# Ordering the high parts of weights behind copies and evictions on ScalarE, and the first layer's value columns as single chunks

## The chip, the cores and the metric

The kernel runs on one core of one Trainium2 chip. Five engines work beside each other and meet only through semaphores: TensorE (PE in the profile, with its weight loads as PEld), VectorE (DVE), ScalarE (ACT), GpSimd (POOL) and SyncE (SP, which here only issues DMAs). [...] The metric is the time of one execution on the device in microseconds; the time before is the median of three runs.

## The reference, cut to what matters

Two layers run over 256 positions with a model width of 2048, all in float32. A layer is

```python
proj = rms_norm(x, mix_norm[l]) @ w_in[l]           # 2048 x 7680: q 1024 | k,v 512 | u 1024 | v 1024 | gates 4096
branch_a = sliding_window_attention(rope(q), rope(k), v, sinks[l]) @ w_attn_branch[l]
branch_b = chunked_sgu(gelu(uv), w_spatial[l], ...) @ w_sgu_branch[l]
merged = sigmoid(gates_a) * branch_a + sigmoid(gates_b) * branch_b
x = x + merged @ w_out[l]
h2 = rms_norm(x, ffn_norm[l])
x = x + (silu(h2 @ w_gate[l]) * (h2 @ w_up[l])) @ w_down[l]     # width 5632
```

Nearly all of the arithmetic is the product of 256 rows with weights that are read from memory once.

## The kernel before, in words

**Entries.** The weights are cut into columns of 512 (a chunk) and these into pieces of 256 rows, 512 KB each. A piece is an *entry*: it is loaded by a DMA that SP issues (L199), split by ACT into a rounded high part (`whi`, L222) and by DVE into the rest (`wlo`, L223), and multiplied by PE with the transposed activations, which are split in the same way (`uh`, `ul`). Of the four partial products three are taken, so one 128x256x512 product is six matmuls (L310 to L312 for two values of `kk`). An ordinary entry is multiplied with both halves of the rows and has twelve. There are four buffers each for `whi` and `wlo`; the program splits an entry four places ahead of its use (`W_SPLIT`), so the high part of entry k+4 takes the buffer that entry k gives back.

**Singles and pairs.** A *single* takes one chunk in eight entries (or four, where the inner width is 1024). A *pair* takes two chunks at once and treats one block of them by the Strassen-Winograd scheme: instead of eight products of that block it has seven, P1 to P7, each an entry of six matmuls, six of which are the *head* of the pair. For that DVE forms four differences of weight pieces (L210), and after P5 two copies on ACT have to move banks: `kept<-acc` (L333) and `acc<-acc` (L334, bank a[1] into bank a[0]). P2 adds to a[0] and cannot begin before L334. After P6 and after P7, DVE reads bank a[1] (`kept`, L336), and nothing may be added to a[1] until it has. Later ACT puts the kept sums into the second pair of banks (L339).

**Order on PE.** PE's instructions run in the order in which they are written. The head of a pair is woven into the last entries of the chunk before it. With t the last entries of that chunk and h the head P1, P5, P2, P6, P7, P4, the order is t0 h0 t1 h1 t2 t3 h2 h3 t4 h4 t5 h5. For a pair that follows a chunk of only four entries (the gate chunks 5 and 6, after the first chunk of the spatial branch, once in each layer) it is t0 h0 t1 h1 t2 h2 h3 t3 h4, and h5 comes after the pair's own first entry.

**Order on the other engines.** ACT, DVE and the DMA queues are ordered by the scheduler of the compiler, before anything runs. Work beside the products (norms, rotary, scores, softmax, gelu, transposes) is put in by `after(n, ...)` and comes due at every twelfth matmul or so (`tick`). `tc.issue_after(ins)` binds everything traced inside it to come later than `ins` on the engine of `ins`. A transposition goes by DVE blocks (`box`, L380), sixteen small DMAs (L385, issued by SP for q, k, the attention and the spatial branch, by POOL elsewhere), and copies on ACT that turn the result into `uh` (L403, L407) or `qT` (L703).

**First part of a layer.** The chunks of `w_in` come in the order of `FIRST_PART[l]`. Layer 0: kv, q0, q1, gate 0, each as a single, then the pairs (v0, v1), (gate 1, u0), (u1, gate 2), (gate 3, gate 4). Layer 1 has (q1, gate 0) as a pair too. Finished banks are evicted by ACT: gates, q and kv at L885, u and v at L776.

Of the kernel before, what the change touches and what calls it, by code (L numbers as in the profile page):

```python
# [1 line left out]

# [8 lines left out]
AF = mybir.ActivationFunctionType  # L11
# [35 lines left out]
Q_FIRST = 17  # L47
Q_STEP = 5
LOAD_BY = (1, 3, 4, 4)
FIRST_PART = [[(("kv", 0),), (("q", 0),)] + early + [(("v", 0), ("v", 1)), (("gate", 1), ("u", 0)), (("u", 1), ("gate", 2)),  # L50
              (("gate", 3), ("gate", 4))]
              for early in ([(("q", 1),), (("gate", 0),)], [(("q", 1), ("gate", 0))])]
GELU_A = 0.044715
GELU_C = 0.7978845608028654

# [2 lines left out]
def hybrid_trunk(ctx: ExitStack, tc: tile.TileContext, x, mix_norm, w_in, q_norm, k_norm, sinks,  # L58
                 sgu_ln_g, sgu_ln_b, w_spatial, b_spatial, w_attn_branch, w_sgu_branch, w_out,
                 ffn_norm, w_gate, w_up, w_down, cosine, sine, out):  # L60
    nc = tc.nc
# [15 lines left out]
    def nm(s):  # L77
        names[0] += 1
        return f"{s}_{names[0]}"

    def slot(shape, dt=F32, name="s"):
        return big.tile(shape, dt, tag="s4", name=nm(name))
# [13 lines left out]
    class Plan:  # L96


        def __init__(self, key, head, body):
            self.key, self.head, self.body = key, head, body  # L100
            self.left = len(head) + len(body)
            self.paired = bool(head)
            self.opened, self.acc, self.calls = set(), {}, None
            for e in head + body:
                e["plan"] = self
            for e in body:
                if e["tag"] == "G":
                    self.last_g = e
# [7 lines left out]
    def half(w, h, tag):  # L116
        ld = load_of(w, h)
        return dict(tag=tag, h=h, loads=[ld], src=ld[0])
# [33 lines left out]
    for l in range(DEPTH):  # L152
        wl = w_in[l]

        def of_in(kind, c):
            o = {"kv": O_KV, "q": 0, "v": O_V, "u": O_U, "gate": O_GATE}[kind] + c * CW
            return wl[:, o:o + CW]

        for f in FIRST_PART[l]:
            plans.append((single if len(f) == 1 else pair)(("in", l), *(of_in(*c) for c in f)))  # L160
# [11 lines left out]
    entries = []  # L172
    for p in plans:
        if p.head:
            h, n = p.head, min(6, len(ahead.body))
            t = [entries.pop() for _ in range(n)][::-1]
            if n == 6:
                entries += [t[0], h[0], t[1], h[1], t[2], t[3], h[2], h[3], t[4], h[4], t[5], h[5]]
            else:
                entries += [t[0], h[0], t[1], h[1], t[2], h[2], h[3], t[3], h[4]]  # L180
                p.body.insert(1, h[5])
        entries += p.body
        ahead = p

    class Stream:
# [1 line left out]


        def __init__(self):
            self.raws, self.parts = {}, []  # L190
            self.asked = self.summed = self.at = 0

        def load(self, upto):
# [20 lines left out]
        def split(self, upto):  # L214
            while len(self.parts) < min(upto, len(entries)):
                e = entries[len(self.parts)]
                raw = self.raws[e["src"]]
                hi = wsp.tile([P, 2, CW], F32R, tag="hi", name=nm("whi"))
                lo = wsp.tile([P, 2, CW], F32R, tag="lo", name=nm("wlo"))
                one = len(self.parts) < 2  # L220
                for i in ([slice(0, 1), slice(1, 2)] if one else [slice(0, 2)]):
                    nc.scalar.activation(hi[:, i, :], raw[:, i, :], AF.Copy)  # L222
                    self.last = nc.vector.tensor_tensor(out=lo[:, i, :], in0=raw[:, i, :], in1=hi[:, i, :].bitcast(F32),  # L223
                                            op=ALU.subtract)
                self.parts.append((hi, lo))
# [8 lines left out]
    stream = Stream()  # L234
# [8 lines left out]
    def tick():  # L243
        slot_no[0] += 1
        due = [s for s in steps if s[0] <= slot_no[0]]
        steps[:] = [s for s in steps if s[0] > slot_no[0]]
        for _, fn in sorted(due, key=lambda s: s[0]):
            with tc.issue_after(stream.last.ins):
                fn()
# [39 lines left out]
    def block(units, h, t):  # L289

        k, tt = 2 * (h % 2), slice(t * P, (t + 1) * P)
        return units[h // 2][0][:, k:k + 2, tt], units[h // 2][1][:, k:k + 2, tt]

    def banks(p, which):
        if which not in p.acc:
            other = p.paired and p.key[0] != "in" and which == "a"
            if other or p.key[0] == "in":
                odd[0] = other and not odd[0]
            pool, tag = (ps_at, "at") if other and odd[0] else (ps_acc, "acc")
            p.acc[which] = [pool.tile([P, CW], F32, tag=tag, name=nm("acc")) for _ in range(NT)]  # L300
        return p.acc[which]

    def add_product(p, ps, u, w):

        (uh, ul), (hi, lo) = u, w
        first = id(ps) not in p.opened
        p.opened.add(id(ps))
        for kk in range(2):
            a, b = uh[:, kk, :], ul[:, kk, :]
            nc.tensor.matmul(ps, a, hi[:, kk, :], start=first and kk == 0, stop=False, skip_group_check=True)  # L310
            nc.tensor.matmul(ps, a, lo[:, kk, :], start=False, stop=False, skip_group_check=True)  # L311
            nc.tensor.matmul(ps, b, hi[:, kk, :], start=False, stop=kk == 1, skip_group_check=True)  # L312

    def step():
        e = entries[stream.at]
        p, tag = e["plan"], e["tag"]
        units = units_at[p.key]
        w = stream.next()
        if tag in "XGU":
            ps = banks(p, "b" if tag == "U" else "a")  # L320
            todo = [(ps[t], block(units, e["h"], t)) for t in range(NT)]
        else:
            sh, sl = units[WINO][2:]
            which, t, form = {"P1": ("a", 1, (0, 0)), "P2": ("a", 0, (1, 0)), "P6": ("a", 1, 1), "P7": ("a", 1, 2),
                              "P4": ("a", 1, (1, 1)), "P5": ("a", 0, 0), "P3": ("b", 0, 3)}[tag]
            todo = [(banks(p, which)[t], (sh[:, form], sl[:, form]) if isinstance(form, int)
                     else block(units, 2 * WINO + form[0], form[1]))]
        for ps, u in todo:
            add_product(p, ps, u, w)
        a, b = p.acc.get("a"), p.acc.get("b")  # L330
        if tag == "P5":
            p.kept = slot([P, 2, CW], name="kept")
            nc.scalar.activation(p.kept[:, 1, :], a[0], AF.Copy)  # L333
            nc.scalar.activation(a[0], a[1], AF.Copy)  # L334
        elif tag in ("P6", "P7"):
            nc.vector.tensor_tensor(out=p.kept[:, int(tag == "P7"), :], in0=a[1], in1=p.kept[:, 1, :], op=ALU.add)  # L336
        if "then" in e:
            for t, ps in enumerate(banks(p, "b")):
                nc.scalar.activation(ps, p.kept[:, t, :], AF.Copy)  # L339
                p.opened.add(id(ps))  # L340
        p.left -= 1
        if e is getattr(p, "last_g", None):
            p.calls[0](a)
        if p.left == 0 and p.paired:
            p.calls[1](b)
        debt[0] += len(todo)
        if debt[0] >= 2:
            debt[0] -= 2
            if p.left or p.paired:
                tick()  # L350
# [7 lines left out]
    def product(key):  # L358

        p = run(key)  # L360
        while p.left:
            step()
        return p.acc["a"]
# [151 lines left out]
    norm = Norm(first_cols)  # L515
# [249 lines left out]
    class Spatial:  # L765
# [6 lines left out]
        def half(self, ps, name):  # L772

            dst = slot([P, NT, CW], name=name)
            for t in range(NT):
                nc.scalar.activation(dst[:, t, :], ps[t], AF.Copy, scale=self.nrm.rh[t])  # L776
            return dst

        def gelu(self, dst, t):
# [90 lines left out]
    for l in range(DEPTH):  # L870
# [6 lines left out]
        def taken(kind, c):  # L877

            def by(ps):
                if kind in ("v", "u"):  # L880
                    (spa.v if kind == "v" else spa.u)(c, ps)
                    return
                dst = slot([P, NT, CW], name=kind)
                for t in range(NT):
                    nc.scalar.activation(dst[:, t, :], ps[t], AF.Tanh if kind == "gate" else AF.Copy,  # L885
                                         scale=(norm.rh if kind == "gate" else norm.r)[t])
                if kind == "gate":
                    gates[c] = dst
                else:
                    att.keys(dst) if kind == "kv" else att.queries(c, dst)  # L890
            return by
# [7 lines left out]

        for chunks in FIRST_PART[l]:  # L900
            projected(*chunks)


        for j in range(NCH):
            ps = product(("att", l))
# [8 lines left out]
        for j in range(NCH):  # L914
            if j == 1:
                projected(("gate", 5), ("gate", 6))
            ps = product(("sgu", l))
# [12 lines left out]
        norm = residual(("mix", l), nxt, scale=0.5)  # L930
# [23 lines left out]
        for r, (f0, f1) in enumerate(ROUNDS):  # L954
# [5 lines left out]
            elif l + 1 < DEPTH:  # L960
                norm = Norm(mix_cols(l + 1), True)
# [41 lines left out]
```

## Time and profile before

| what | value |
|---|---|
| median of three runs | 2497.29 us (2497.01 to 2497.77) |
| the profiled execution's own time | 2497.96 us |
| its span, first to last instruction | 2496.3 us |
| PE busy | 2468.9 us, 99% |
| DVE busy | 1950.6 us, 78% |
| ACT busy | 1442.4 us, 58% |
| POOL busy | 286.1 us, 11% |
| mean granted TensorE clock | 0.997 |

The profile comes from one execution. A row of the timeline gives the start, the duration, the engine, the source line, what is written from what, the number of merged instructions, and in brackets how long the engine had been idle before it and what ended the idle time. Matmuls are pipelined: a row's duration of 0.39 us is longer than the distance to the next one.

### The profile page before, as it was taken

To read this page: it belongs to the slowest core of one execution; us is meant where nothing else is said; L and a number is where in the kernel's file an instruction comes from. 1 tells how busy PE (TensorE), PEld (TensorE's weight loads), DVE (VectorE), ACT (ScalarE), POOL (GpSimd) and SP (SyncE) were. 2 spreads that over 40 slices of the span, in tenths; PEclk is the share of its full clock that TensorE was granted. 3 is DMA by queue.
4 is the path that set the end of the run, shared out by engine and by line. 5 is a ranking of instruction groups with operands and counts; after the bars stand their busy time and mean duration, and the time that the engine had idled before them with its cause. 6 is when DMAs were issued, how large, how long until landed. Compare 5 with 4: busy or idle time off the path is not lost.

```text
span 2496.3 us, 31305 instructions
## 1 busy us (share of the span) xinstructions
PE 2468.9 (99%) x11076; PEld 2029.9 (81%) x11076; DVE 1950.6 (78%) x2279; ACT 1442.4 (58%) x1808; POOL 286.1 (11%) x527
## 2 busy tenths in 40 slices
PE   9999999999999999999999999999999999999999
PEld 7788888788888888888888888787888888888887
DVE  6888676787877787778878986767878777877786
ACT  5576544565655565556656665445655555655564
POOL 3100002131110111001101000112211101110110
PEclk9999999999999999999999999999999999999999
DMA  8565567566665757566657546665767566666664
GB/s 292 175 190 166 194 194 223 182 211 219 191 230 170 227 186 233 179 214 205 217 157 247 170 159 222 205 198 181 230 194 223 193 207 196 218 203 192 214 193 151
DMA packets 275661, 502.54 MB, mean 201 GB/s; under 512 B 26224, under 2 KB 36048, under 8 KB 275504
## 3 DMA queue, kind: packets, MB, share of 16 engines
q1 hardware_dynamic: 259472, 484.25, 61.1%
q0 software_dynamic: 15712, 16.01, 2.2%
q8 instruction: 87, 1.43, 0.2%
q14 instruction: 70, 0.57, 0.1%
q10 hardware_dynamic: 320, 0.27, 0.0%
HBM read 475.27 MB, written 2.10 MB: 191 GB/s over the span
## 4 chain that ended last, share of the span: by engine, by line
PE 93%; DVE 4%; issue 1%; ACT 1%; DMA 1%; SPq 0%; DVEq 0%; ACTq 0%
PE acc L310 30%; PE acc L311 30%; PE acc L312 30%; DVE wlo L223 2%; PE po L758 1%; DVE raw L210 1%; PE pt L421 1%; DMA raw<-in_w_in_dram 0%; PE psc L719 0%; SPq L385 0%; PE ppt L748 0%; ACT whi L222 0%; PE psg L836 0%; DVE pr L723 0%; DVE kept L336 0%
## 5 line engine op out<-in xcount | busy, mean ns | idle before, releaser
L223 DVE TENSOR_TENSOR wlo<-raw,whi 128x1024 fp32r<-128x1024 f32 (+1 forms) x1045 | 1272.8, 1220 | 488.9 <-ACT whi L222 474.2
L222 ACT ACTIVATE whi<-raw 128x1024 fp32r<-128x1024 f32 (+1 forms) x1045 | 1103.6, 1058 | 950.6 <-PE acc L312 768.1
L310 PE MATMUL acc<-whi,uh 128*128 128x512 f32 x3094 | 1211.3, 391 | 15.6 <-ACT acc L334 10.8
L311 PE MATMUL acc<-wlo,uh 128*128 128x512 f32 x3094 | 1205.8, 390 | 0.9 <-DVE wlo L223 0.8
L312 PE MATMUL acc<-whi,ul 128*128 128x512 f32 x3094 | 1205.9, 390 | 0.0
L310 PEld LDWEIGHTS acc<-whi,uh 128*128 128x128 f32 x3094 | 581.6, 188 | 138.0 <-ACT acc L334 12.0
L311 PEld LDWEIGHTS acc<-wlo,uh 128*128 128x128 f32 x3094 | 581.8, 188 | 122.6 <-DVE wlo L223 3.0
L312 PEld LDWEIGHTS acc<-whi,ul 128*128 128x128 f32 x3094 | 581.4, 188 | 121.7
L385 POOL DMA_DIRECT2D tt<-box x480 | 235.2, 497 | 1721.5 <-DVE box L380 573.2
L210 DVE TENSOR_TENSOR raw<-raw,raw 128x1024 f32<-128x1024 f32 x196 | 239.1, 1220 | 1.4
L310 PE MATMUL acc<-whi,sh 128*128 128x512 f32 x392 | 158.5, 404 | 4.5 <-DVE kept L336 3.6
L311 PE MATMUL acc<-wlo,sh 128*128 128x512 f32 x392 | 154.3, 394 | 0.8 <-DVE wlo L223 0.8
L312 PE MATMUL acc<-whi,sl 128*128 128x512 f32 x392 | 154.2, 393 | 0.0
L310 PEld LDWEIGHTS acc<-whi,sh 128*128 128x128 f32 x392 | 74.3, 190 | 32.2 <-issue 12.3
L312 PEld LDWEIGHTS acc<-whi,sl 128*128 128x128 f32 x392 | 74.4, 190 | 15.9
L311 PEld LDWEIGHTS acc<-wlo,sh 128*128 128x128 f32 x392 | 74.5, 190 | 15.0 <-DVE wlo L223 1.1
L336 DVE TENSOR_TENSOR kept<-acc,kept 128x512 f32<-128x512 f32 x98 | 67.0, 684 | 0.4 <-PE acc L312 0.4
L339 ACT ACTIVATE acc<-kept 128x512 f32<-128x512 f32 x98 | 56.6, 588 | 9.5 <-DVE kept L336 9.2
L853 DVE SCALAR_TENSOR_TENSOR xs<-acc,xs 128x512 f32<-128x512 f32 (+1 forms) x66 | 41.4, 667 | 7.8 <-PE acc L312 7.8
L942 ACT ACTIVATE hid<-acc,rhalf 128x512 f32<-128x512 f32 x44 | 30.4, 690 | 21.0 <-PE acc L312 21.0
L943 DVE SCALAR_TENSOR_TENSOR hid<-hid,acc 128x512 f32<-128x512 f32 x44 | 29.8, 684 | 9.3 <-ACT hid L942 9.3
L333 ACT ACTIVATE kept<-acc 128x512 f32<-128x512 f32 x49 | 29.1, 595 | 13.0 <-PE acc L312 13.0
(135 smaller groups left out, 885.2 us busy)
## 6 DMA issues: line engine op xcount, KB each, us to landing
raw<-in_w_in_dram SPq DMA_DIRECT2D x239, 512.0 KB, 4.6
raw<-in_w_up_dram SPq DMA_DIRECT2D x176, 512.0 KB, 4.8
raw<-in_w_gate_dram SPq DMA_DIRECT2D x176, 512.0 KB, 4.6
raw<-in_w_down_dram SPq DMA_DIRECT2D x176, 512.0 KB, 4.6
raw<-in_w_out_dram SPq DMA_DIRECT2D x64, 512.0 KB, 4.7
raw<-in_w_attn_branch_dram SPq DMA_DIRECT2D x32, 512.0 KB, 5.4
raw<-in_w_sgu_branch_dram SPq DMA_DIRECT2D x32, 512.0 KB, 4.2
tt<-box POOLq DMA_DIRECT2D x480, 32.0 KB, 4.2
```

The source lines that it names most:

```text
L210: self.last = nc.vector.tensor_tensor(out=self.raws[d], in0=self.raws[x], in1=self.raws[y], op=ALU.subtract)
L222: nc.scalar.activation(hi[:, i, :], raw[:, i, :], AF.Copy)
L223: self.last = nc.vector.tensor_tensor(out=lo[:, i, :], in0=raw[:, i, :], in1=hi[:, i, :].bitcast(F32), op=ALU.subtract)
L310: nc.tensor.matmul(ps, a, hi[:, kk, :], start=first and kk == 0, stop=False, skip_group_check=True)
L311: nc.tensor.matmul(ps, a, lo[:, kk, :], start=False, stop=False, skip_group_check=True)
L312: nc.tensor.matmul(ps, b, hi[:, kk, :], start=False, stop=kk == 1, skip_group_check=True)
L336: nc.vector.tensor_tensor(out=p.kept[:, int(tag == "P7"), :], in0=a[1], in1=p.kept[:, 1, :], op=ALU.add)
L339: nc.scalar.activation(ps, p.kept[:, t, :], AF.Copy)
L385: queue.dma_start(dst[j * B:(j + 1) * B, i], box[i * B:(i + 1) * B, j])
L853: nc.vector.scalar_tensor_tensor(out=xs[:, t, sl], in0=sums[t][:, i * w:(i + 1) * w], scalar=scale, in1=xs[:, t, sl], op0=ALU.mult, op1=AL ...
L942: nc.scalar.activation(th, g[t], AF.Tanh, scale=norm.rh[t])
L943: nc.vector.scalar_tensor_tensor(out=th, in0=th, scalar=1.0, in1=g[t], op0=ALU.add, op1=ALU.mult)
```

## The change

There are three edits. First, the stream of weights remembers an ACT instruction, `stream.urgent`: the last L334 copy, or the last eviction of q, gate, u or v (not of kv). Each high part traced after it (L222) is bound to come behind it on ACT. Second, in layer 0 the value chunks v0 and v1 are two singles instead of one pair. Third, where a pair follows a chunk of four entries, the head begins one entry earlier and ends before the pair's own first entry.

```diff
-FIRST_PART = [[(("kv", 0),), (("q", 0),)] + early + [(("v", 0), ("v", 1)), (("gate", 1), ("u", 0)), (("u", 1), ("gate", 2)),
-              (("gate", 3), ("gate", 4))]
-              for early in ([(("q", 1),), (("gate", 0),)], [(("q", 1), ("gate", 0))])]
+FIRST_PART = [[(("kv", 0),), (("q", 0),)] + early + [(("gate", 1), ("u", 0)), (("u", 1), ("gate", 2)), (("gate", 3), ("gate", 4))]
+              for early in ([(("q", 1),), (("gate", 0),), (("v", 0),), (("v", 1),)],
+                            [(("q", 1), ("gate", 0)), (("v", 0), ("v", 1))])]
...
-                entries += [t[0], h[0], t[1], h[1], t[2], h[2], h[3], t[3], h[4]]
-                p.body.insert(1, h[5])
+                entries += [h[0], t[0], h[1], t[1], h[2], h[3], t[2], h[4], t[3], h[5]]
...
-            self.raws, self.parts = {}, []
+            self.raws, self.parts, self.urgent = {}, [], None
...
-                    nc.scalar.activation(hi[:, i, :], raw[:, i, :], AF.Copy)
+                    with tc.issue_after(self.urgent.ins) if self.urgent else nullcontext():
+                        nc.scalar.activation(hi[:, i, :], raw[:, i, :], AF.Copy)
...
-            nc.scalar.activation(a[0], a[1], AF.Copy)
+            stream.urgent = nc.scalar.activation(a[0], a[1], AF.Copy)
...
-                nc.scalar.activation(dst[:, t, :], ps[t], AF.Copy, scale=self.nrm.rh[t])
+                stream.urgent = nc.scalar.activation(dst[:, t, :], ps[t], AF.Copy, scale=self.nrm.rh[t])
...
-                    nc.scalar.activation(dst[:, t, :], ps[t], AF.Tanh if kind == "gate" else AF.Copy,
-                                         scale=(norm.rh if kind == "gate" else norm.r)[t])
+                    last = nc.scalar.activation(dst[:, t, :], ps[t], AF.Tanh if kind == "gate" else AF.Copy,
+                                                scale=(norm.rh if kind == "gate" else norm.r)[t])
+                    if kind != "kv":
+                        stream.urgent = last
```

## The prediction on record

> **What bounds the kernel now.** PE is busy for 2468.9 of 2496.3 us, so I read its waits first, then the timeline around each.
>
> ```profile
> PE acc L310 <- ACT acc L334: 10.8, 3, 4.1
> PE acc L310 <- DVE kept L336: 6.8, 6, 1.6
> ```
>
> PE's waits by what ended them: us in total, times, longest. Three waits for the bank copy L334 are the largest item, six for the reads L336 the next.
>
> ```profile
> 92.34 0.51 PE L310 MATMUL acc<-whi,sh 128*128 128x512 f32 x1 [0.28 <-ACT whi L222]
> 93.60 0.50 PE L311 MATMUL acc<-wlo,sh 128*128 128x512 f32 x1 [0.75 <-DVE wlo L223]
> ...
> 100.08 0.39 PE L312 MATMUL acc<-whi,ul 128*128 128x512 f32 x1
> 104.57 0.79 PE L310 MATMUL acc<-whi,uh 128*128 128x512 f32 x1 [4.11 <-ACT acc L334]
> ...
> 109.99 0.88 PE L719 MATMUL psc<-kT,qT 64*128 64x128 f32 x8
> ```
>
> This is layer 0, where the head of (v0, v1) is woven into gate 0. PE loses 0.28 and 0.75 us on P5's weights and 4.11 us on L334, and then works slowly.
>
> ```profile
> 460.40 0.39 PE L311 MATMUL acc<-wlo,uh 128*128 128x512 f32 x1
> 460.63 0.39 PE L312 MATMUL acc<-whi,ul 128*128 128x512 f32 x1
> 464.35 0.50 PE L310 MATMUL acc<-whi,uh 128*128 128x512 f32 x1 [3.33 <-ACT acc L334]
> ```
>
> The same before P2 of the first `w_out` pair, woven into gate 7. The first two rows give PE's pitch, 0.23 us; I use 0.227. The third wait is what is left of 10.8: 10.8 - 4.11 - 3.33 = 3.4 us, the same place in layer 1.
>
> Between 104.57 and 109.99 us stand twelve matmuls (P2 and P6); at 0.227 they would take 2.72 us, they took 5.42: 2.7 us more. For the other place the windows show it:
>
> ```profile
> 350.00:375.00 25.00, 23.43 (x103) 18.85 (x101) 21.77 (x23) 13.13 (x14) 0.00 (x0) 1.00 0.49 154
> ...
> 450.00:475.00 25.00, 21.67 (x89) 17.43 (x88) 17.41 (x18) 13.23 (x15) 5.16 (x11) 0.93 0.60 184
> ```
>
> The last but two number is the granted clock. A mean of 0.93 over 25 us is a loss of 1.75 us. In the other window PE idled too (1.57 us) and the clock stayed at 1.00. So the copies cost 4.11 + 2.7 in layer 0's first part and 3.33 + 1.75 = 5.1 in front of each `w_out` stage.
>
> **The value chunks as singles.** The head of (v0, v1) goes, and with it its waits: 0.28 + 0.75 + 4.11 + 2.7 = 7.8 us. The scheme saved one of eight products; its six matmuls come back: 6 x 0.227 = 1.4 us. Off PE there are fewer operations (16 splits instead of 19, no L210, L333, L334, L336, L339), which costs nothing. What is late next? The scores need `qT`:
>
> ```profile
> 101.46 1.15 ACT L703 ACTIVATE qT<-tt 128x512 f32<-128x512 f32 x2 [1.25 <-DMA tt<-box]
> 102.51 0.58 ACT L333 ACTIVATE kept<-acc 128x512 f32<-128x512 f32 x1
> 102.99 1.04 ACT L222 ACTIVATE whi<-raw 128x1024 fp32r<-128x1024 f32 x1
> 103.94 0.59 ACT L334 ACTIVATE acc<-acc 128x512 f32<-128x512 f32 x1
> ```
>
> Here is the reason of the 4.11 us: L333 and L334 stood on ACT behind L703, which waited for the sixteen small DMAs. Their removal brings PE to the scores at 109.99 - 7.8 = 102.2 us, and L703 ends at 102.6: 0.4 us is given back. An earlier eviction of q may bring L703 forward (then 0), a later gather may hold it; I take +0.3, bounds 0 and 1.25, the wait that ACT shows here.
>
> ```profile
> 90.03 10.01 SPq L385 DMA_DIRECT2D tt<-box  x16
> ```
>
> ```profile
> raw<-in_w_in_dram SPq DMA_DIRECT2D x239, 512.0 KB, 4.6
> ```
>
> SP's queue is held for 10.0 us by this gather, and the loads of the singles stand behind it. A piece is loaded into one of five buffers; a buffer that comes free when entry k+4 is split serves entry k+9, whose product begins 8 x 12 x 0.227 = 21.8 us after entry k. Taking off a split at either end (2.3 us each, below) leaves 17.2, against 10.0 for the gather and 4.6 for a load to land: nothing, with 2.6 us to spare. The part comes to -7.8 + 1.4 + 0.3 = -6.1 us.
>
> **The earlier head in front of gates 5 and 6.**
>
> ```profile
> 371.96 0.68 DVE L923 SCALAR_TENSOR_TENSOR gate<-gate,acc 128x512 f32<-128x512 f32 x1
> ...
> 374.30 0.69 DVE L336 TENSOR_TENSOR kept<-acc,kept 128x512 f32<-128x512 f32 x1
> ```
> ```profile
> 375.04 0.50 PE L310 MATMUL acc<-whi,uh 128*128 128x512 f32 x1 [1.61 <-DVE kept L336]
> ```
> ```profile
> 1610.35 0.50 PE L310 MATMUL acc<-whi,uh 128*128 128x512 f32 x1 [1.61 <-DVE kept L336]
> ```
>
> After P7 bank a[1] may not be touched until L336 has read it; only six matmuls (1.36 us) lie between, and the evictions of the spatial chunk (L923) reached DVE just before. With the new order twelve matmuls of that chunk (2.72 us) follow P7, and its evictions can't come before they end. I take both waits as gone, -3.2 us. New is that the spatial chunk's first entry follows the attention chunk's last by six matmuls, 1.36 us, and needs the bank two chunks back: an eviction like L923 (0.68 us) behind a split in progress (1.22 us) takes 1.9, so up to 0.54 us a layer. I take 0.2: -2.8 us, bounds -3.2 and 0.
>
> **The high parts behind the copies.** In front of `w_out`:
>
> ```profile
> 461.10 1.06 ACT L222 ACTIVATE whi<-raw 128x1024 fp32r<-128x1024 f32 x1 [1.66 <-PE acc L312]
> 462.06 1.13 ACT L403 ACTIVATE uh<-tt 128x512 fp32r<-128x512 f32 x2
> 463.10 0.58 ACT L333 ACTIVATE kept<-acc 128x512 f32<-128x512 f32 x1
> 463.71 0.58 ACT L334 ACTIVATE acc<-acc 128x512 f32<-128x512 f32 x1
> ```
> ```profile
> 453.06 2.93 POOL L385 DMA_DIRECT2D tt<-box x6 [0.83 <-DMA tt<-box]
> ```
> ```profile
> tt<-box POOLq DMA_DIRECT2D x16, 32.0 KB, 4.0
> ```
>
> L222 at 461.10 waits for PE's last entry before P2 (it needs that entry's buffer), and everything behind it waits along. Bound behind L334, this and two high parts before it get out of the way. But L403 stands ahead of L333 as well, and the diff doesn't touch it. It waits for the gather, whose last issue ends at 455.99 and which takes 4.0 us to land: 460.0. Then L403 twice, L333 and L334 end at 462.3, and PE, ready at 460.86, waits 1.4 us instead of 3.33. The price stands behind: three high parts now follow L334.
>
> ```profile
> L223 DVE TENSOR_TENSOR wlo<-raw,whi 128x1024 fp32r<-128x1024 f32 (+1 forms) x1045 | 1272.8, 1220 | 488.9 <-ACT whi L222 474.2
> L222 ACT ACTIVATE whi<-raw 128x1024 fp32r<-128x1024 f32 (+1 forms) x1045 | 1103.6, 1058 | 950.6 <-PE acc L312 768.1
> ```
>
> A split takes 1.06 + 1.22 = 2.3 us. The first is ready at 464.6 and P6 wants its low part at 463.9: 0.7 us. The second, behind a difference of pieces on DVE (1.22, like a split), is ready near 467.0, wanted near 466.0: 1.0 us. So 3.1 us of waiting stands against 5.1 of waiting and slow clock: -2.0 us a layer, -4.0 in all. Bounds: nothing gained (the waits long enough to slow the clock again, 1.75), and 5.1 a layer, if L333 gets ahead of L403 too.
>
> [...]
>
> At the other pairs:
>
> ```profile
> 2342.24 1.23 DVE L223 TENSOR_TENSOR wlo<-raw,whi 128x1024 fp32r<-128x1024 f32 x1 [1.46 <-ACT whi L222]
> ...
> 2345.66 0.68 DVE L336 TENSOR_TENSOR kept<-acc,kept 128x512 f32<-128x512 f32 x1
> ```
>
> The high part that now runs between L333 and L334 will run after L334, 0.59 us later. The low part moves with it, but DVE idles 1.46 us before the next but one, ahead of L336: 0. At evictions:
>
> ```profile
> 60.81 1.06 ACT L222 ACTIVATE whi<-raw 128x1024 fp32r<-128x1024 f32 x1 [1.66 <-PE acc L312]
> 63.53 1.06 ACT L222 ACTIVATE whi<-raw 128x1024 fp32r<-128x1024 f32 x1 [1.66 <-PE acc L312]
> 64.50 1.25 ACT L885 ACTIVATE q<-acc,rstd 128x512 f32<-128x512 f32 x2
> ```
>
> q is evicted behind high parts of the following chunk. In the new order it goes first and each high part comes 1.25 us later; it has three entries of PE's time, 36 x 0.227 = 8.2 us, less 2.3 for the split: 5.9 us to spare, so 0. The rest of the L336 row, 6.8 - 3.2 = 3.6 us in four waits, shifts with DVE's order; with less work on DVE in layer 0 I take -0.3, bounds -3.6 and +2.4 (four times 0.59).
>
> **Sum.** -6.1 - 2.8 - 4.0 - 0.3 = -13.2 us. The profiled execution took 2497.96 us, 1.7 outside its span; 2484.8 after. The median shown is 0.67 lower: **2484.1 us**. The terms' distances to their bounds, as the root of their squares (down 0.3, 0.4 and 3.3; up 0.95, 2.8, 4.0 and 2.7), give this case 2481 to 2490.
>
> **Rivals.** (1) The copies get ahead of L403 too and the waits in front of `w_out` vanish: 6.2 us more, 2477.9. For it: L333's bank was full when P5 ended, 24 matmuls (5.4 us) before 460.86, so it was not PE that held it. Against: L403 precedes it now, and is not bound. (2) In front of `w_out` nothing is won, since three high parts behind a waiting L403 starve PE as long as before: 2488.1. For it: L703 above, which shows ACT idle 1.25 us on a DMA with ready work behind it. [...] (3) The scores, or the next pair's P5, meet the second q gather as P5 met the first: 4.11 + 2.7 come back, 2490.9. Against: a single has no P5. (4) Slower: the 0.59 us by which high parts come later reaches L336. Six calls of L336 end too late already, so others may end just in time; it decides at the point where DVE's idle time ahead of it (1.46 us here) is under 0.59. At 49 pairs (98 calls of L336) it costs 49 x 0.59 = 28.9 us: 2513. Against: that idle time. (5) The edits cancel, or the order comes out as it was: within 5 us of 2497.3.
>
> **Chances.** Forecast 0.46; (1) 0.12; (2) 0.18; (3) 0.05; (4) 0.13; (5) 0.06. A measurement of this kernel tells about 0.2% (5 us) from no change. Faster: 0.46 + 0.12 + 0.18 + 0.05 = 0.81; same 0.06; slower 0.13. The range holds the first four cases, with a little more than 1 us of margin below (1) and above (3): 2476.5 to 2492.
>
> **What would show it.** In the profile after: no wait for L334 over 2 us and a clock of 1.00 in the windows around 95 and 455 us; PE's waits for `wlo` growing by 1 to 2 us in front of `w_out`; no wait for L336 before gates 5 and 6; q's evictions ahead of high parts; 98 - 2 calls of L336 and 1042 splits. The forecast is wrong if waits for `whi`, `wlo` or L336 turn up in the ordinary pairs, or a new wait for `qT` exceeds 1 us.

## The result and the profile after

The changed kernel takes 2494.51 us (median of 20 runs) against 2497.84 us of the kernel before (20 runs beside them): a ratio of 0.9987, 95% interval 0.998 to 0.9993. It is 3.3 us faster, where 13.2 were forecast. Its profiled execution took 2496.61 us with a span of 2494.9 us, one of the slower ones of the 20 (2492.69 to 2496.76). PE's waits in it, grouped by what ended them (total, times, longest):

```profile
PE acc L310 <- DVE kept L336: 8.8, 11, 2.4
PE acc L311 <- DVE wlo L223: 4.9, 11, 0.8
PE acc L310 <- ACT acc L334: 2.4, 2, 1.3
PE acc L310 <- DVE negm L729: 1.8, 1, 1.8
```

The waits for L334 fell from 10.8 to 2.4 us, as the change meant. Those for L336 grew from 6.8 to 8.8, and from six to eleven, although the two of 1.61 us before gates 5 and 6 are gone. The wait put down to L729 belongs to them too (below). The timeline of PE shows where they stand:

```profile
81.14 0.50 PE L310 MATMUL acc<-whi,uh 128*128 128x512 f32 x1 [0.59 <-ACT whi L222]
82.40 0.50 PE L311 MATMUL acc<-wlo,uh 128*128 128x512 f32 x1 [0.76 <-DVE wlo L223]
...
161.93 0.64 PE L310 MATMUL acc<-whi,sh 128*128 128x512 f32 x1 [2.36 <-DVE kept L336]
...
457.96 0.50 PE L310 MATMUL acc<-whi,uh 128*128 128x512 f32 x1 [1.27 <-ACT acc L334]
460.19 0.50 PE L311 MATMUL acc<-wlo,sh 128*128 128x512 f32 x1 [0.34 <-DVE wlo L223]
462.46 0.50 PE L311 MATMUL acc<-wlo,uh 128*128 128x512 f32 x1 [0.62 <-DVE wlo L223]
466.70 0.47 PE L310 MATMUL acc<-whi,sh 128*128 128x512 f32 x1 [1.45 <-DVE kept L336]
...
765.97 0.47 PE L310 MATMUL acc<-whi,sh 128*128 128x512 f32 x1 [0.21 <-DVE kept L336]
...
1397.90 0.76 PE L310 MATMUL acc<-whi,sh 128*128 128x512 f32 x1 [1.77 <-DVE negm L729]
```

The windows add the clock (last but two number):

```profile
150.00:175.00 25.00, 22.64 (x115) 18.08 (x114) 23.42 (x43) 16.16 (x28) 1.01 (x1) 0.93 0.56 169
...
450.00:475.00 25.00, 21.32 (x91) 16.32 (x90) 19.04 (x21) 14.59 (x18) 1.97 (x5) 1.00 0.58 186
```

In front of `w_out` the clock is whole again (1.00). Behind the 2.36 us wait it is now halved (0.50 from 162.07 to 165.48 us; 0.93 over 25 us is 1.75 us lost), and around the end of the 1.77 us wait too (0.50 from 1397.69 to 1401.10 us).

**Where the time went.** PE executes the same matmuls in both kernels (six more in layer 0), so the start of the same matmul in both timelines, subtracted, gives what was won or lost up to there; the difference of two such numbers is a stage. The columns after "after" are experiments told below; all stages are against the profiled execution of before, in us; 224 to 354 is left out, with 0.1 us or less in all seven.

| stage (times of before) | after | e1 | e3 | e4 | e5 | e9 | e11 |
|---|---|---|---|---|---|---|---|
| start, to 48 | +0.7 | -0.6 | 0.0 | -0.2 | +0.5 | -0.6 | -0.2 |
| head of (v0, v1), first gather, to 95 | +0.4 | -1.6 | -0.5 | -1.6 | -1.6 | -1.4 | -1.6 |
| values to the scores, to 143 | -6.1 | -6.1 | -2.9 | -6.1 | -5.6 | -6.0 | -6.0 |
| behind the first scores, to 224 | +2.6 | -0.6 | -0.9 | -0.7 | -0.6 | +2.6 | +2.1 |
| gates 5 and 6, 354 to 424 | -1.9 | 0.0 | 0.0 | -1.9 | -1.9 | -1.9 | -1.9 |
| `w_out`, to 519 | -0.5 | +1.3 | -2.3 | 0.0 | -1.5 | -0.7 | -1.2 |
| feed-forward, to 1176 | +0.7 | +1.4 | +0.7 | +1.4 | +0.7 | +0.7 | +0.7 |
| first part of layer 1, to 1607 | +5.3 | +3.0 | +0.9 | +4.1 | +5.2 | +5.9 | +4.2 |
| gates 5 and 6, to 1677 | -1.9 | 0.0 | 0.0 | -1.9 | -1.9 | -1.9 | -1.9 |
| `w_out`, to 1726 | -0.5 | 0.0 | -0.7 | -1.6 | -2.3 | -0.6 | -1.0 |
| to 1840 | -1.3 | -1.3 | -1.1 | -1.3 | -1.3 | -1.3 | -1.3 |
| feed-forward, to the end | +1.2 | +0.5 | +1.1 | +0.4 | +1.1 | +1.1 | +1.1 |

For after the stages add up to -1.3 us; the profiled execution is 2.1 us above the median. Most of two of the forecast's three parts is there: -6.1 us between 95 and 143, -3.8 at gates 5 and 6. In front of the two `w_out` only 1.0 of 4.0 us came, and +2.6 at the first scores and +5.3 in the first part of layer 1 were given back, places that the prediction had put at nothing.

### The profile page after: what moved, and what is told of

Read it like the earlier page. It is cut to its first block, busy times and chain, and to the rows that moved or that the text cites. A ratio compares the mean times of both kernels' runs of the same rounds, so it can differ in the third digit from the quotient of the medians.

```text
span 2494.9 us, 31270 instructions
## 1 busy us (share of the span) xinstructions
PE 2468.9 (99%) x11082; PEld 2028.4 (81%) x11082; DVE 1941.6 (78%) x2270; ACT 1440.1 (58%) x1801; POOL 286.7 (11%) x527
## 5 line engine op out<-in xcount | busy, mean ns | idle before, releaser
L222 ACT ACTIVATE whi<-raw 128x1024 fp32r<-128x1024 f32 (+1 forms) x1042 | 1099.1, 1058 | 926.0 <-PE acc L312 739.3
L336 DVE TENSOR_TENSOR kept<-acc,kept 128x512 f32<-128x512 f32 x96 | 65.6, 683 | 0.5 <-PE acc L312 0.5
L404 DVE TENSOR_TENSOR ul<-tt,uh 128x512 fp32r<-128x512 f32 x44 | 28.9, 684 | 12.4 <-ACT uh L403 12.4
```

The lines of the kernel that those rows point to most:

```text
L404: nc.vector.tensor_tensor(out=l, in0=s_, in1=h.bitcast(F32), op=ALU.subtract)
```

## The experiments

Two theories stood at the start. **Theory 1:** the price of the new order lies at the copies L334; the high part behind a copy is late, its low part with it, and L336 stands behind that on DVE. **Theory 2:** either the singles, or the evictions, shift DVE's order, and the copies are worth what was forecast. Ratios are against the kernel before, run beside each on the same chip; a difference is from that kernel's median there.

| kernel | what it has | us | ratio, 95% interval | difference |
|---|---|---|---|---|
| e1 | singles | 2492.93 | 0.9981 (0.9972 to 0.999) | -5.0 |
| e2 | heads | 2495.06 | 0.9988 (0.9979 to 0.9997) | -2.9 |
| e3 | order at copies and evictions | 2494.16 | 0.9987 (0.9978 to 0.9995) | -3.8 |
| e4 | singles, heads | 2491.23 | 0.9972 (0.9961 to 0.9983) | -6.7 |
| e5 | singles, heads, copies | 2487.14 | 0.996 (0.9948 to 0.9973) | -10.4 |
| e6 | singles, heads, evictions | 2496.14 | 0.9995 (0.9986 to 1.0004) | -1.4 |
| c_copies | copies | 2496.14 | 0.9997 (0.9988 to 1.0005) | -1.4 |
| c_evict | evictions | 2496.25 | 0.9996 (0.9987 to 1.0005) | -1.3 |
| e7 | e5, copies of `w_out` alone | 2486.94 | 0.9959 (0.9946 to 0.9971) | -10.5 |
| e8 | after without q's evictions | 2487.87 | 0.996 (0.9948 to 0.9973) | -9.6 |
| e9 | e5 with q's evictions | 2493.89 | 0.9985 (0.9976 to 0.9994) | -3.6 |
| e10 | e5 with q0's in layer 0 | 2490.43 | 0.9972 (0.9961 to 0.9983) | -7.0 |
| e11 | e5, L727 ahead of the first L336 | 2491.34 | 0.9973 (0.9962 to 0.9983) | -6.3 |
| e12 | e5 with q1's in layer 0 | 2493.8 | 0.9984 (0.9975 to 0.9993) | -3.8 |

### The parts alone: e1 to e4

e1 is the first hunk of the diff alone, e2 the second, e3 all that touches `urgent`, e4 the first two.

> Only the value chunks of layer 0 as singles. Theory 1 (the trace of the changed kernel lost its gain through the new order of the high parts: longer waits for L336 after the scores of both layers): without that order the part gives what its stage gave in the trace, -6.1 us, so ratio 0.9976; PE's wait for L336 behind the first (gate 1, u 0) product stays near the 1.31 us that it had, with the clock at 1.00. Theory 2 (the singles themselves shift DVE's order in layer 0 and so make that wait long): the wait is 2 us or more, half the clock follows it, and the part gives -6.1 + 2.7 = -3.4 us, ratio 0.9986.

> Only the head one entry earlier in front of gates 5 and 6. Both theories: the two 1.61 us waits for L336 go and nothing takes their place: -3.2 us by the waits, -3.8 us by the steps of the changed kernel's trace (-1.87 and -1.91 between the same PE instructions), ratio 0.9985 to 0.9987; no wait for the bank, and no other wait changes.

> Only the order on ScalarE, at copies and evictions. Theory 1: the changed kernel's -3.3 us less -6.1 and -3.8 leaves +6.6 us for this part, ratio 1.0026: about -0.5 us in front of each output stage, about +0.25 us in each of a few ordinary pairs, and several us through waits for L336 behind the scores. Theory 2: +3 to +4 us, ratio 1.0014, with the long wait of layer 0 absent. The prediction had -4.0 us, ratio 0.9984.

> The first two parts without the order on ScalarE. Theory 1: -6.1 - 3.8 = -9.9 us, ratio 0.9960, faster than the changed kernel by 6.6 us. Theory 2: -3.4 - 3.8 = -7.2 us, ratio 0.9971.

e1 came out between the two theories in time, with the short wait (0.74 us) behind the first scores that theory 1 had; e2 a little under what was expected, e4 near the number of theory 2 without its long wait. Both theories were wrong on e3: the order alone is worth -3.8 us, where both had it slower than before. Its gain overlaps with that of the singles: -2.9 us of it is the same wait for L334 in layer 0. What is left over is not an overlap, though: e4 without the order (-6.7) beats the changed kernel (-3.3). The singles alone gave -7.7 us up to 143 and lost 3.0 in layer 1, whose lists of chunks the edit leaves as they were (below); the wait of 0.74 us behind the first scores stayed short, with a stage of -0.6 us for the changed kernel's +2.6, so it isn't the singles that make it long.

### Copies against evictions: e5, e6, c_copies, c_evict

```diff
 e5: only this of the `urgent` lines, with singles and heads (c_copies: without them)
+            stream.urgent = nc.scalar.activation(a[0], a[1], AF.Copy)
 e6: only these, with singles and heads (c_evict: without them)
+                stream.urgent = nc.scalar.activation(dst[:, t, :], ps[t], AF.Copy, scale=self.nrm.rh[t])
+                    if kind != "kv":
+                        stream.urgent = last
```

> Values as singles, heads earlier, and high parts behind the bank copies L334 alone (evictions free). Theory 1 (the price of the order lies at the copies: the high part behind L334 is late by a copy, its low part stands ahead of L336 on DVE): the 0.21 us waits for L336 in ordinary pairs are there (seven, some 0.3 us each with the restart of PE, 2.1 us), the long wait for L336 behind the first scores is there (2 us or more, half the clock behind it in some executions), the four short waits in front of the output stage are there (-0.5 us a layer): about 2494 us, ratio 0.9985. Theory 2 (the price lies at the evictions): no long wait behind the first scores, about 2490.5 us, ratio 0.9970.

> Values as singles, heads earlier, and high parts behind the evictions of q, v, u and gate alone (copies free). Theory 1: no 0.21 us waits for L336, the 3.33 us waits for L334 in front of the output stage stay, and only layer 0's first loads are late (waits for whi and wlo near 81 us, some 1.9 us with restarts): about 2492.5 us, ratio 0.9978. Theory 2: the long wait behind the first scores and the waits near 81 us are both there: 2494.5 us or more, ratio 0.9986.

> The kernel before with high parts behind the copies L334 alone. It has the 4.11 us wait of layer 0 to win as well (-2.9 us in the trace with the whole order), and the price of theory 1 (2.1 us in ordinary pairs): theory 1 2495 us, ratio 0.9990; theory 2 2493 us, ratio 0.9980, as the evictions' price is missing.

> The kernel before with high parts behind the evictions alone. All three waits for L334 stay (3.3 to 4.1 us each). Theory 1: within 2 us of before, 2496 to 2500 us. Theory 2: slower by 2 to 4 us, ratio 1.0008 to 1.0016.

Theory 1 falls for the kernel with singles and heads. With the copies alone it is at 2487.14 us, 10.4 us faster than before and better than either theory had it; with the evictions alone e4's gain is nearly all gone (+5.3 us to e4). On top of e5 the evictions cost 10.4 - 3.3 = 7.1 us. Without singles and heads (c_copies, c_evict) neither part can be told from no change: c_copies is 1.1 us above theory 1's number and 3.1 above theory 2's, and c_evict is where theory 1 had it. So the evictions' price belongs to the combination, and not to the evictions alone. The price that theory 1 spoke of exists but is small: e5 has the 0.21 us waits. Its waits:

```profile
PE acc L311 <- DVE wlo L223: 4.7, 10, 0.8
PE acc L310 <- DVE kept L336: 3.0, 9, 0.8
PE acc L310 <- ACT acc L334: 2.2, 2, 1.1
PE acc L310 <- DVE negm L729: 1.8, 1, 1.8
```

Against the changed kernel, L336 is down from 8.8 to 3.0 us. By the table, the 7.9 us between the two profiles are 2.0 at the first gather, 3.2 behind the first scores (+2.6 against -0.6), 2.8 in front of the two output stages, and little else.

### Which eviction: e7 to e10

```diff
 e7:
-            stream.urgent = nc.scalar.activation(a[0], a[1], AF.Copy)
+            copied = nc.scalar.activation(a[0], a[1], AF.Copy)
+            stream.urgent = copied if p.key[0] == "mix" else None
 e8 (L776 as in the change):
-                    if kind != "kv":
+                    if kind == "gate":
 e9 (L776 as before):
-                    if kind != "kv":
+                    if kind == "q":
 e10 (L776 as before; e12 with c == 1):
-                    if kind != "kv":
+                    if kind == "q" and l == 0 and c == 0:
```

> Values as singles, heads earlier, and high parts behind the copies L334 of the output pairs alone. By the traces the copies of the other pairs only cost: six or seven waits for L336 of 0.21 us, 0.3 us each between the same PE instructions, 2.1 us in all. If that is so: 2487.1 - 2.1 = 2485.0 us, ratio 0.9950, no wait of 0.21 us, and the four short waits in front of the first output stage as they were. Rival (the copies elsewhere gain as much as they cost, in the first part of layer 1): 2487 us or more.

> The changed kernel with only the evictions of q taken out of the order; those of v, u and gate, and the copies, stay in. Theory q (the whole price of the evictions comes from q's in layer 0): 2487 us, ratio 0.996, the wait for L336 behind the first scores 0.7 us, no wait near 81 us. Rival (v's evictions make the long wait, since they sit where the high parts of that pair are due): 2491 to 2494 us with the 2.36 us wait. In this kernel's program order on VectorE L336 stands ahead of the row maximum L727, as without any evictions, which speaks for theory q.

> The version with singles, early heads and copies, and of the evictions those of q alone. Theory q: as slow as the changed kernel, 2494.5 us, ratio 0.9987, with the 2.36 us wait for L336 near 162 us and waits for whi and wlo near 81 us. Rival: 2487 to 2489 us, only the waits near 81 us.

> The version with singles, early heads and copies, and of the evictions that of q chunk 0 in layer 0 alone. In its program order L336 stands ahead of L727 again, so the long wait near 162 us should be gone and only the late loads near 81 us should be left (0.59 + 0.76 us and PE's restarts, some 1.9 us): 2487.1 + 1.9 = 2489.0 us, ratio 0.9964. If the long wait is a consequence of the late loads it is there, and the time is 2493 us or more.

Theory q holds in the times: taking q out of the order (e8) gives back nearly the whole of e5's time, q alone (e9) takes it away. But neither e9 nor e10 has the waits near 81 us that were expected of them. e10 came out at 2490.4 us for 2489.0, and not by the late loads that the 1.9 us stood for: the wait behind the scores is short as expected (0.79 us), but in front of the second `w_out` L336 is late by 1.45 us, and that stage is 2.1 us worse than e5's. e7 missed its 2485.0 us: it lost all the 0.21 us waits and won nothing that its median shows; one wait of 1.01 us for L336 that e5 lacks came back at 546.80 us.

What the order does at q, from ACT's timeline of the changed kernel:

```profile
57.47 0.69 ACT L885 ACTIVATE q<-acc,rstd 128x512 f32<-128x512 f32 x1 [0.30 <-PE acc L312]
58.83 0.69 ACT L885 ACTIVATE q<-acc,rstd 128x512 f32<-128x512 f32 x1 [0.67 <-PE acc L312]
62.05 0.91 ACT L448 ACTIVATE flat<-tt,first_cols 128x256 f32<-128x256 f32 x2 [2.53 <-DMA tt<-box]
62.87 1.04 ACT L222 ACTIVATE whi<-raw 128x1024 fp32r<-128x1024 f32 x1
```

In before, three high parts stand ahead of q's eviction at 64.50, the last at 63.53. Now q goes first, and the next high part stands behind L448 too, which waits 2.53 us for small DMAs of the transposition. So pieces are given back later, and on SP's queue (start, duration, line, number of DMAs):

```profile
51.60 7.23 SPq L198 DMA_DIRECT2D raw<-in_w_in_dram  x4
63.49 10.09 SPq L385 DMA_DIRECT2D kT<-box  x16
...
74.32 1.75 SPq L198 DMA_DIRECT2D raw<-in_w_in_dram  x3
```

Four loads are out before the gather takes the queue for 10.1 us; in e5 there are six. The first load behind it is split at 80.03, and PE waits 0.59 and 0.76 us. Whether this costs anything differs. e9 and e10 have four loads ahead of the gather too, but there L448 waited only 1.03 and 1.07 us, the first load behind the gather was split at 76.94 and 77.90, and PE didn't wait. The stage to 95 is -1.6 us in all six kernels with singles and without q's evictions, and between -1.4 and +0.4 in the five with both. So the late loads are 2.0 us of the changed kernel's profile, but only 0.2 of what q costs in e9.

### The place of L336: e11, e12

The wait behind the first scores. PE's timeline of the changed kernel, the last matmul of P7 and the last one ahead of the wait:

```profile
156.46 0.39 PE L312 MATMUL acc<-whi,sl 128*128 128x512 f32 x1
...
159.18 0.39 PE L312 MATMUL acc<-whi,ul 128*128 128x512 f32 x1
```

DVE's timeline of the same kernel:

```profile
157.64 1.22 DVE L209 TENSOR_TENSOR raw<-raw,raw 128x1024 f32<-128x1024 f32 x1
158.77 1.21 DVE L727 TENSOR_REDUCE mx<-pr 128x4 f32<-128x1024 f32 x1
159.90 1.21 DVE L223 TENSOR_TENSOR wlo<-raw,whi 128x1024 fp32r<-128x1024 f32 x1
161.03 0.16 DVE L804 TENSOR_SCALAR ve<-mv 128x4 f32<-128x4 f32 x1
161.10 0.68 DVE L336 TENSOR_TENSOR kept<-acc,kept 128x512 f32<-128x512 f32 x1
```

and of e5:

```profile
156.51 1.21 DVE L223 TENSOR_TENSOR wlo<-raw,whi 128x1024 fp32r<-128x1024 f32 x1
157.65 0.68 DVE L336 TENSOR_TENSOR kept<-acc,kept 128x512 f32<-128x512 f32 x1
...
158.31 1.21 DVE L727 TENSOR_REDUCE mx<-pr 128x4 f32<-128x1024 f32 x1
```

P7 ended near 156.9 us, and L336, which reads its bank, could have run from then on; PE needed it from 159.6 (161.93 - 2.36). But the compiler had put a difference of pieces, the row maximum L727 and a low part ahead of it, and DVE works through them without a pause. In e5 the maximum stands behind. PE's order is the same in the two kernels; DVE's differs in 151 of its 2270 places, and six of the 96 calls of L336 stand elsewhere, up to three places later. In e8, without q's evictions, all 96 stand as in e5. To test that place alone, e11 binds the first L336 behind the maximum, with no eviction in the order:

```diff
-            nc.vector.tensor_reduce(out=mx, in_=pr4[:, :, :nk], axis=AX.X, op=ALU.max)
+            top = nc.vector.tensor_reduce(out=mx, in_=pr4[:, :, :nk], axis=AX.X, op=ALU.max)
+            if stream.top is not False:
+                stream.top = top
...
-            nc.vector.tensor_tensor(out=p.kept[:, int(tag == "P7"), :], in0=a[1], in1=p.kept[:, 1, :], op=ALU.add)
+            with tc.issue_after(stream.top.ins) if stream.top else nullcontext():
+                nc.vector.tensor_tensor(out=p.kept[:, int(tag == "P7"), :], in0=a[1], in1=p.kept[:, 1, :], op=ALU.add)
+            stream.top = False
```

> The fast version (singles, early heads, copies; no evictions) with one thing added: the first L336 of layer 0 is bound behind the row maximum L727 on VectorE, as the program order of the changed kernel has it. Nothing else ahead of it differs; no high part and no load moves. If the place of L336 in VectorE's order makes the loss, the wait of 0.69 us near 158 us becomes 0.69 + 1.13 (the maximum) + 0.1 = 1.9 us, and the kernel is slower by 1.2 us, or by 2.9 where half the clock follows: 2488.4 to 2490.1 us, ratio 0.9964 to 0.9971. If the late high parts make it, the wait stays near 0.7 us and the time at 2487.1.

> The fast version with the eviction of q chunk 1 in layer 0 alone in the order. Its program order has L727 ahead of L336 as the changed kernel's, but q chunk 0 and the loads around the first gather are as in the fast version. Theory (the place of L336): a wait of about 1.9 us near 160 us, none near 81 us, and 2488.4 to 2490.5 us. Rival (q chunk 0 makes the whole price, through late loads): 2487 us.

e11's DVE and PE (its lines are one and two further down, L729 is the maximum and L337 the read):

```profile
156.75 1.22 DVE L729 TENSOR_REDUCE mx<-pr 128x4 f32<-128x1024 f32 x1
157.88 0.68 DVE L337 TENSOR_TENSOR kept<-acc,kept 128x512 f32<-128x512 f32 x1
```
```profile
158.72 0.47 PE L310 MATMUL acc<-whi,sh 128*128 128x512 f32 x1 [1.89 <-DVE kept L337]
```

The wait is 1.89 us, for 1.9 expected, and half the clock follows (a mean of 0.93 from 150 to 175 us): the stage goes from -0.6 to +2.1, 2.8 us. The rival for this place (late high parts) falls. But the kernel is 4.1 us slower than e5, not 2.9: in the second `w_out` L336 is now late by 1.45 us as well. One edge in layer 0 had moved that L336 three places down DVE's order in layer 1, behind a low part, a difference and another low part. e12 has the same at the scores, with a low part ahead too, as in the changed kernel: a wait of 3.25 us, and 2493.8 us in place of 2488.4 to 2490.5. So q0 alone (e10, +3.3 us to e5) and q1 alone (e12, +6.6) each cost, with different displacements.

The first part of layer 1 has a late L336 as well. DVE of before, and then of e1, whose edit is in layer 0 only:

```profile
1394.41 1.21 DVE L223 TENSOR_TENSOR wlo<-raw,whi 128x1024 fp32r<-128x1024 f32 x1
1395.54 0.47 DVE L800 BATCH_NORM_STATS2 bst<-v 128x6 f32<-128x128 f32 x2
1395.94 1.10 DVE L812 TENSOR_SCALAR v<-v,mv,rv 128x128 f32<-128x128 f32 x4
1396.96 0.68 DVE L336 TENSOR_TENSOR kept<-acc,kept 128x512 f32<-128x512 f32 x1
```
```profile
1388.94 1.22 DVE L223 TENSOR_TENSOR wlo<-raw,whi 128x1024 fp32r<-128x1024 f32 x1
1390.07 1.22 DVE L210 TENSOR_TENSOR raw<-raw,raw 128x1024 f32<-128x1024 f32 x1
1391.21 0.87 DVE L800 BATCH_NORM_STATS2 bst<-v 128x6 f32<-128x128 f32 x4
1391.99 0.68 DVE L820 TENSOR_TENSOR v<-v,ln 128x512 f32<-128x512 f32 x1
1392.58 1.22 DVE L223 TENSOR_TENSOR wlo<-raw,whi 128x1024 fp32r<-128x1024 f32 x1
1393.72 0.69 DVE L336 TENSOR_TENSOR kept<-acc,kept 128x512 f32<-128x512 f32 x1
1394.32 0.15 DVE L729 SCALAR_TENSOR_TENSOR negm<-mx,nsnk 128x4 f32<-128x4 f32 x1
```

PE's timeline of the two, from the last matmul of P7 to the wait:

```profile
1393.15 0.39 PE L312 MATMUL acc<-whi,sl 128*128 128x512 f32 x1
1393.38 1.00 PE L758 MATMUL po<-kv,pT 128*128 128x64 f32 x8
...
1397.78 0.47 PE L310 MATMUL acc<-whi,sh 128*128 128x512 f32 x1 [0.59 <-DVE kept L336]
```
```profile
1388.84 0.39 PE L312 MATMUL acc<-whi,sl 128*128 128x512 f32 x1
...
1391.78 1.00 PE L758 MATMUL po<-kv,pT 128*128 128x64 f32 x8
1394.55 0.47 PE L310 MATMUL acc<-whi,sh 128*128 128x512 f32 x1 [1.77 <-DVE negm L729]
```

L336 begins 3.4 us after P7's end in before and 4.5 us after it in e1, behind other work, and PE waits 1.77 us for it instead of 0.59 (the row names L729, which ended last by 0.1 us and has nothing to do with the bank). In the eleven kernels with singles this stage costs 3.0 to 6.1 us, in the four without (e2, e3, c_copies, c_evict) 0.1 to 0.9. All eleven lose 1.1 us at this wait, 0.7 near 1353 and 0.9 to 1.2 at transposes on PE near 1236; nine of them also lose about 1.6 to a stretch of half clock (in e5 the mean from 1375 to 1400 us is 0.93). That the singles bring the loss is shown.

What brings it is not settled, for the written order had moved too. The two singles have one product of six matmuls more than the pair, half an entry. The program counts entries for `tick` and carries the remainder on, so the side work of layer 1 comes due at other matmuls: in the rows above, the eight L758 stand behind P7 in before and one entry later in e1. PE's timelines show such shifts, up to twelve matmuls, in layer 1 of all eleven kernels with singles and in none of the four without. Whether the loss comes from these shifts or from the places that the compiler gave L336, no edit of layer 1 has tested.

## Why the prediction was wrong, point by point

- **What bounds the kernel:** right. What the stages won and lost, beside the six matmuls more, stands in PE's waits and the slow clock behind them.
- **Singles, -6.1 us:** right at its place, even small: -7.7 in e1 (the stages -1.6 and -6.1), no wait for `qT`. Its cost in layer 1 (+3.0 in e1) had no term: the sum counted the six matmuls at their place and not that they shift the side work behind. By medians -5.0.
- **Earlier head, -2.8 us:** right: -2.9 by medians, -3.8 by stages, no new wait for the bank. A wait of 1.61 us was worth 1.87 to 1.91.
- **Order in front of `w_out`, -4.0 us:** the steps held (L334 1.27 for 1.4, low parts 0.34 and 0.62 for 0.7 and 1.0, the clock 1.00), and with the copies alone the two stages give -3.8 (e5). That waits of 1.4, 0.7 and 1.0 us leave the clock whole, on which 1.75 us a layer of the sum rest, was the author's estimate, which no trace of before shows; the changed kernel had 1.27, 0.34 and 0.62 us and a clock of 1.00 from 450 to 475 us. That the sum is so near is partly luck: e5's waits there are 2.3 and 2.0 us and not 3.1, but there are three or four short stops in place of one long one, and each costs more than its idle time (last section). In the changed kernel the two stages give -1.0: PE waits 1.45 us for L336 behind P6, which the sum left out, since DVE's order has one more low part ahead of it in layer 0 and two and a difference in layer 1.
- **Other pairs, 0:** too low. Rival (4) is real at a tenth of its price or less: six waits of 0.21 us, some 0.3 each between the same matmuls, 2 us and not 28.9.
- **Evictions, 0: this is the step that failed.** That a high part "has three entries of PE's time" and so "5.9 us to spare" counted PE's distance alone. It left out above all that the compiler orders DVE anew: with q's evictions in the order L336 stands behind the row maximum at the first scores (a wait of 2.36 us and half the clock, 3.2 us) and behind more low parts in front of `w_out` (2.8 us). It also left out L448, which stands on ACT with the high parts behind it and waits for DMAs, and the buffers given back later, whose loads fall behind the gather on SP (2.0 us in the changed kernel's profile, 0.2 in e9's). The price of the evictions is 7.1 us on top of e5, of which q alone takes 6.8 (e9).
- **The rest of L336, -0.3 with bounds -3.6 and +2.4:** the bounds were too narrow. They took DVE's order as given; it was not. The -1.3 us of the stage to 1840 belong here: a wait of 1.02 us for L336 at 1793.44, which before, e2 and c_evict have and the others don't.

For what the edits unsettle the sum had 2.4 us upward, in the L336 term. The version without the failed step, e5, is at 2487.14 us, 3.0 above the forecast; e5, e7 and e8 are the fastest of all (0.996, 0.9959 and 0.996 of before).

Open is why the compiler chooses these places, and whether the loss in layer 1 would go if `tick` kept its old count or L336 its old place there: nothing ran that kept either.

## What to carry to other kernels

Where a compiler orders the engines, a binding in one queue is not a local edit: look for the one short instruction on another engine that the bounding engine waits for (L336 here, 0.68 us), compare its place in that engine's order before and after, and price each place lost at the length of the instruction put ahead of it (in e11 the maximum, 1.22 us, took a wait of 0.69 us to 1.89). "So much time to spare" is only an answer if it is counted along every queue that the moved work shares, with the waits for DMAs that stand in it. A count that the program carries on, like that of `tick`, takes an edit to places far behind it, so compare the bounding engine's written order first. Time the parts of a change in combination: these three gave -5.0, -2.9 and -3.8 alone and -3.3 together.

## What the runs showed of the hardware

**The length of a wait didn't settle the clock.** In the traces of before and of the changed kernel the granted clock fell to 0.50 around the end of these waits of PE: 4.11 us in before (0.50 from 103.54 to 110.37 us), 3.33 us twice in before (465.36 to 468.77, 1700.98 to 1704.39), 2.36 and 1.77 us in the changed kernel (162.07 to 165.48, 1397.69 to 1401.10). At the start of before it was 0.50 from 7.97 to 11.38 us, just behind a wait of 1.50 us for `uh` that ended at 7.77; the prediction passed over this when it read that trace. Around a wait of 1.89 us in e11 (150 to 175 us) and one of 1.77 us in e5 (1375 to 1400 us) the mean was 0.93. It was 1.00 around the wait of 1.61 us in before at 375.04 (350 to 400 us), around one of 1.76 us in e9 (1375 to 1400 us), and around one of 3.33 us in e4; its PE and windows:

```profile
1692.70 0.50 PE L309 MATMUL acc<-whi,uh 128*128 128x512 f32 x1 [3.33 <-ACT acc L333]
```
```profile
1675.00:1700.00 25.00, 21.67 (x96) 17.61 (x95) 18.93 (x20) 13.06 (x16) 7.82 (x16) 1.00 0.54 169
1700.00:1725.00 25.00, 25.00 (x116) 20.81 (x115) 19.63 (x22) 14.96 (x20) 0.00 (x0) 1.00 0.63 207
```

So in the same place of layer 1 a wait of 1.77 us in e5 came with half the clock and one of 1.76 us in e9 without, and 3.33 us in front of `w_out` did in before and not in e4. What decides was not shown. A stretch of 3.41 us at 0.50 is about 1.7 us lost, an estimate from the stretches above; how much of the scatter between executions that is was not worked out.

**A stop of PE costs more than its idle time.** Waits of 1.61 us that went were worth 1.87 to 1.91 us between the same matmuls, and one of 0.21 costs 0.3: an idle time is counted from the end of a matmul, 0.39 us after its start, and without a stop the next one starts after 0.23.
